# Storing the modulated input of the second block, and splitting projection inputs in the tile they are loaded into

## The chip, the cores and the metric

The kernel runs on one core of a Trainium2 chip. The metric is the time of one execution on the device in microseconds, as the median of several runs. The engines of a core run side by side, each through its own row of instructions in a fixed order: TensorE (PE, matmuls), VectorE (DVE), ScalarE (ACT), GpSimd (POOL) and SyncE (SP). In this kernel SP and POOL do hardly anything but issue transfers between the chip's memory and the core's tiles, and 16 DMA engines carry them out.

## The reference

One decoder layer for a sequence of 2048 tokens of width 1024, in float32. A conditioning vector gives a shift, a scale and a gate per channel for each of two sub-layers.

```python
def reference(x, c, w_ada, b_ada, w_in, conv_w, w_pool, pool_scale, w_out, ...):
    ...
        sh1, sc1, g1, sh2, sc2, g2 = jnp.split(mod, N_MOD, axis=-1)   # mod = silu(c) @ w_ada + b_ada
        h = x * (1.0 + sc1) + sh1            # the modulated input of this case
        z = h @ w_in[l]                      # 1024 -> 2048: the input projection
        ...                                  # gated short convolution and causal pooling of z
        mix = jnp.concatenate([y_conv, y_pool], axis=-1) @ w_out[l]
        x = _layer_norm(DEEPNORM_ALPHA * x + (1.0 + g1) * mix, ln1_g[l], ln1_b[l])
        h = x * (1.0 + sc2) + sh2
        f = jnp.square(jax.nn.relu(h @ w_mlp_in[l])) @ w_mlp_out[l]   # 1024 -> 4096 -> 1024
        x = _layer_norm(DEEPNORM_ALPHA * x + (1.0 + g2) * f, ln2_g[l], ln2_b[l])
```

The change touches how `h` of the first sub-layer gets into the product with `w_in`, for the second half of the tokens.

## The kernel before

**Blocks.** The 2048 tokens are worked on in two blocks of 1024 (`T`, `NB` = 2), one after the other: input projection with convolution and pooling, output projection and norm, MLP up, MLP down and norm. `xT` holds the input transposed, 8 tiles (`KD`) of 128 channels by 1024 tokens.

**Digits.** Every float32 operand is split into a high part, the value rounded to the format that PE takes (`F32R`), and a low part, what is left. A product is three matmuls in `mm3`: high by high (L153), high weight by low input (L154), low weight by high input (L155), each 128x128 by 128x512. `split` (and `parts`, for weights) makes the two: a cast on ACT (L146) and a subtraction on DVE (L147). So a weight tile costs a cast and a low part, and PE reads the low part from the third matmul on.

**Seven products.** The large matrix products are done in 2x2 blocks with seven block products in place of eight, as Strassen and Winograd do it. `seven` runs them in the order 0 to 6 in which they are called; one is 24 matmuls into two PSUM banks. The price is sums: of weight blocks, of input blocks and of results, made by DVE. In the MLP's first matrix (`up`) the hidden units come in 8 groups `g` (`NC` = 8). After each product `up` empties the banks with copies (`keep`, L1086), additions (`add`) or directly with an activation (`c21`, L1180, whose square is L1181); `join` is followed by the activation and the square, L1098 and L1099. The results' sums go to `usum` through POOL's queue.

**Tiles.** Tiles come from pools of fixed size, and one that asks for a slot waits until its last holder was read or stored: 10 for `o` (results and the side jobs), 6 for `w` (weight parts), 5 for `r` (what was loaded and is to be split), 28 for `h` (input parts).

**Side jobs.** The input projection of the second block also needs sums of its input blocks (`xsum`) and of its first weight (`winsum`). They are made while the first block's `up` runs. At the end of every product, `up` calls `beside`, which lets the side jobs advance by one beat: seven beats in a group. `first_side` starts four jobs `sum_x` at the beats 5, 11, 13 and 18 and two jobs `sum_first` at 20 and 26; `timed` starts a job's loads at its beat and runs the rest three beats later. `sum_x(k)` loads two tiles of `xT` into `o` tiles by POOL's queue, modulates them on ACT (L672), makes four differences of 128x512 on DVE in place and stores the two tiles to `xsum` by POOL's queue (L680).

**Preparing.** `prepare` is called through `turn` in the last group (`g` = 7), between its products 4 and 5. It loads and splits the first two weights and the first three inputs of the second block's projection; the further weights and inputs follow while the projection's first products run (`in_proj_1`). `inputs(X, key)` makes two tiles for each key; the keys with two digits are plain blocks (`xT`), those with one digit are sums (`xsum`). The load goes into an `r` tile by SP's queue (L705). A plain block is then modulated twice on ACT, once into the high part and once in place (four activations of 128x512, L712), and DVE subtracts; a sum goes through `split`. SP's queue also carries the weights' loads, L624 for this projection's.

The program that results has each engine's instructions in an order that a scheduler writes; the PE row near the last group's end holds some matmuls of the next projection's first product ahead of that group's product 6.

Of the kernel before, what the change touches and what calls it, by code (L numbers as in the profile page):

```python
# [8 lines left out]
F32 = mybir.dt.float32  # L9
F32R = mybir.dt.float32r  # L10
AF = mybir.ActivationFunctionType
ALU = mybir.AluOpType

P = 128
D = 1024
S = 2048
T = 1024
H = 512
NB = S // T
KD = D // P  # L20
# [80 lines left out]
SC1, SH1 = 0, 1  # L101
# [7 lines left out]
def tile_hybrid_layer(ctx: ExitStack, tc: tile.TileContext, opening, xT, x, wada, win,  # L109
                      wins, wpool, wout, wmix, w1, w2, rows, out):  # L110
    nc = tc.nc
# [11 lines left out]
    def mk(p, shape, dt, tag, bufs):  # L123
        names[0] += 1
        return p.tile(shape, dt, name=f"{tag}_{names[0]}", tag=tag, bufs=bufs)

    def t_h(dt=F32R):
        return mk(big, [P, T], dt, "h", 28)

    def t_o(w=T, dt=F32):  # L130
        return mk(big, [P, w], dt, "o", 10)
# [4 lines left out]
    def t_r():  # L136
        return mk(big, [P, T], F32, "r", 5)
# [7 lines left out]
    def split(src, hi, lo):  # L145
        high = nc.scalar.copy(hi, src)  # L146
        return high.ins, nc.vector.tensor_tensor(lo, src, hi.bitcast(F32), op=ALU.subtract).ins  # L147
# [15 lines left out]
    def tt(out_, a, b_, op):  # L163
        return nc.vector.tensor_tensor(out_, a, b_, op=op)  # L164
# [14 lines left out]
    halves = [slice(h * H, h * H + H) for h in range(2)]  # L179
# [24 lines left out]
    mod = cp.tile([P, 48], F32, name="mod")  # L204
# [46 lines left out]
    gout = tc.dram_tile([2, KD // 2, P, T], F32, name="gout")  # L251
    winsum = tc.dram_tile([4, P, T], F32, name="winsum")
    w1sum = tc.dram_tile([2, 4, P, T], F32, name="w1sum")
    xsum = tc.dram_tile([2, 4, P, T], F32, name="xsum")
    grow = tc.dram_tile([2, D], F32, name="grow")
    msum = tc.dram_tile([7, NG - 1, P, H], F32, name="msum")
# [409 lines left out]
    def sum_x(k):  # L666
        rs = [t_o() for _ in range(2)]
        for i, r in zip((k, k + 4), rs):
            nc.gpsimd.dma_start(r, xT[i])
        yield  # L670
        for i, r in zip((k, k + 4), rs):
            nc.scalar.activation(r, r, AF.Identity, bias=mod[:, 2 * i + SH1 : 2 * i + SH1 + 1],  # L672
                                 scale=mod[:, 2 * i + SC1 : 2 * i + SC1 + 1])
        (b11, b12), (b21, b22) = ((r[:, :H], r[:, H:]) for r in rs)
        tt(b12, b12, b11, ALU.subtract)
        tt(b22, b22, b12, ALU.subtract)
        tt(b11, b22, b11, ALU.subtract)
        tt(b21, b21, b22, ALU.subtract)
        for i, r in enumerate(rs):
            nc.gpsimd.dma_start(xsum[i, k], r)  # L680
# [13 lines left out]

    def inputs(X, key):
        for q in range(2):
            r = t_r()
            X[key, q] = hi, lo = t_h(), t_h()
            if len(key) == 1:
                src, hs = xsum[(int(key) + 1) % 2], halves[int(key) % 4 > 0 and int(key) < 3]  # L700
                k = 2 * q
            else:
                k, hs = 4 * int(key[0]) - 4 + 2 * q, halves[int(key[1]) - 1]
                src = xT
            nc.sync.dma_start(r.rearrange("p (a n) -> p a n", a=2),  # L705
                              src[k : k + 2, :, hs].rearrange("a p n -> p a n"))
            if len(key) == 1:
                split(r, hi, lo)
                continue
            for dst in (hi, r):  # L710
                for a, cs in enumerate(halves):
                    nc.scalar.activation(dst[:, cs], r[:, cs], AF.Identity,  # L712
                                         bias=mod[:, 2 * (k + a) + SH1 : 2 * (k + a) + SH1 + 1],
                                         scale=mod[:, 2 * (k + a) + SC1 : 2 * (k + a) + SC1 + 1])
            tt(lo, r, hi.bitcast(F32), ALU.subtract)

    def prepare():
        X = {}
        W = summed_weights(wins[0], winsum, (0, 1, 5, 4, 6, 7, 3))
        first_w = [parts(next(W), t_w)]  # L720
        for i in range(2):
            inputs(X, ORDER[i][1])
        first_w.append(parts(next(W), t_w))
        inputs(X, ORDER[2][1])
        return X, W, first_w

    def in_proj_1(X, W, first_w):
# [14 lines left out]
        def group(j):  # L742
# [11 lines left out]
            if j == 0:  # L754
                inputs(X, ORDER[3][1])
# [694 lines left out]
    def timed(jobs):  # L1450
        due = {}
        for beat in range(48):
            for _ in due.pop(beat, ()):
                pass
            if beat in jobs:
                next(jobs[beat])
                due[beat + 3] = jobs[beat]
            yield

    def first_side():  # L1460
        sums = [sum_x(n) for n in range(4)] + [sum_first(p) for p in halves]
        return timed(dict(zip((5, 11, 13, 18, 20, 26), sums)))

    def second_side():
        rows_ = [gate_dot(f) for f in range(G2, G2 + KD)] + [gate_row(), gate_back()]
        return timed(dict(zip((4, 6, 11, 13, 18, 20, 25, 27, 33, 37), rows_)))
# [93 lines left out]
```

## Time and profile before

| | |
|---|---|
| median of 3 runs | 1705.51 us (1705.37 to 1707.76) |
| profiled execution | 1707.25 us, of which the span is 1705.5 us |
| mean granted PE clock | 0.997 |
| moved by DMA | 469 MB, 275 GB/s on the mean |
| xsum stores | 8 of 512 KB, from 373.2 to 450.7 us |
| input loads for the second block (L705) | from 548.73 us on |

In the lines below, a row of the timeline has the start, the duration, the engine, the line and the operation with what is written and read; in brackets the idle time before it and what ended it. `x2` says that two such instructions follow each other. Instructions of one engine overlap a little, so the distance of two starts says more of the cost than the duration. A row of the waits has the total, the number and the longest. A row of DMA issues has the size and the median time from issue to landing. DVE is busy for 82% of the span and ACT for 49%, unevenly: the stages with sums fill DVE.

### The profile page before, as it was taken

What the parts mean: (1) busy time and instruction counts of PE and PEld (TensorE: products, weight loads), DVE (VectorE), ACT (ScalarE), POOL (GpSimd) and SP (SyncE); (2) the same over time, 40 slices, a digit from 0 to 9 for tenths busy, and PEclk for the clock granted to TensorE, in tenths of its full rate; (3) what the DMA queues carried; (4) which work ended last, traced back from release to release, by engine and by line L of the source; (5) the groups of instructions that cost most, each with busy time, mean ns of one, the idle gap of its engine ahead of it and who ended that gap; (6) DMA issues with size and microseconds to landing.
All of it is one profiled execution on the core that took longest, in us unless ns stands there. A gap on an engine that the chain in (4) does not pass through costs nothing.

```text
span 1705.5 us, 22025 instructions
## 1 busy us (share of the span) xinstructions
PE 1688.1 (99%) x7519; PEld 1396.8 (82%) x7519; DVE 1399.6 (82%) x2138; ACT 844.2 (49%) x1160; POOL 377.9 (22%) x687
## 2 busy tenths in 40 slices
PE   9999999999999899999999999999999999999998
PEld 7888888888888688888888888888888888888886
DVE  8898697888887586886888788766988887897898
ACT  6323358555554753345855454445543433334555
POOL 0222221445564122200145455430000000000000
PEclk9999999999999999999999999999999999999999
DMA  9998877668778778865889998899899999896782
GB/s 387 346 335 323 312 253 275 224 218 259 241 247 221 228 234 223 238 241 197 267 251 266 243 244 243 240 330 355 317 344 338 384 328 353 292 338 222 264 291 99
DMA packets 149217, 469.47 MB, mean 275 GB/s; under 512 B 20456, under 2 KB 20976, under 8 KB 149104
## 3 DMA queue, kind: packets, MB, share of 16 engines
q1 hardware_dynamic: 93184, 303.38, 50.5%
q0 software_dynamic: 55920, 164.67, 32.0%
q8 instruction: 59, 0.97, 0.3%
q14 instruction: 54, 0.44, 0.1%
HBM read 350.01 MB, written 159.91 MB: 299 GB/s over the span
## 4 chain that ended last, share of the span: by engine, by line
PE 90%; DVE 4%; DMA 3%; ACT 1%; issue 1%; POOL 0%; DVEq 0%; SPq 0%; ACTq 0%; POOLq 0%
PE ps L153 29%; PE ps L155 29%; PE ps L154 29%; PE ps L488 3%; DVE o L164 2%; DMA r<-in_xT 1%; PE ps L865 1%; DMA usum<-o 1%; DVE w L147 1%; DMA w<-in_w 1%; DVE r L164 0%; DMA wsum<-in_w 0%; DMA r<-in_w 0%; POOL usum L1111 0%; ACT w L146 0%
## 5 line engine op out<-in xcount | busy, mean ns | idle before, releaser
L153 PE MATMUL ps<-h,w 128*128 128x512 f32 x1312 | 511.9, 391 | 5.9 <-ACT w L146 4.2
L155 PE MATMUL ps<-h,w 128*128 128x512 f32 x1312 | 511.3, 390 | 0.5 <-DVE w L147 0.5
L154 PE MATMUL ps<-h,w 128*128 128x512 f32 x1312 | 511.7, 390 | 0.0
L153 PE MATMUL ps<-h,h 128*128 128x512 f32 (+1 forms) x1064 | 412.4, 388 | 0.9 <-DVE h L164 0.9
L154 PE MATMUL ps<-h,h 128*128 128x512 f32 (+1 forms) x1064 | 412.4, 388 | 0.9 <-DVE h L147 0.9
L155 PE MATMUL ps<-h,h 128*128 128x512 f32 (+1 forms) x1064 | 412.4, 388 | 0.0
L153 PEld LDWEIGHTS ps<-h,w 128*128 128x128 f32 x1312 | 246.9, 188 | 58.5 <-ACT w L146 4.7
L155 PEld LDWEIGHTS ps<-h,w 128*128 128x128 f32 x1312 | 246.7, 188 | 53.3 <-DVE w L147 1.7
L154 PEld LDWEIGHTS ps<-h,w 128*128 128x128 f32 x1312 | 247.1, 188 | 51.3
L1111 POOL DMA_DIRECT2D usum<-o x416 | 225.2, 550 | 254.2 <-DVE o L164 162.6
L146 ACT CAST w<-r 128x1024 fp32r<-128x1024 f32 x156 | 164.2, 1052 | 196.0 <-PE ps L154 190.4
L147 DVE TENSOR_TENSOR w<-r,w 128x1024 fp32r<-128x1024 f32 x156 | 190.6, 1223 | 59.9 <-ACT w L146 59.1
L146 ACT CAST h<-r 128x1024 fp32r<-128x1024 f32 (+1 forms) x136 | 136.5, 1009 | 198.6 <-PE ps L154 79.6
L154 PEld LDWEIGHTS ps<-h,h 128*128 128x128 f32 x1064 | 199.8, 188 | 42.1 <-DVE h L147 1.3
L153 PEld LDWEIGHTS ps<-h,h 128*128 128x128 f32 x1064 | 199.8, 188 | 42.0 <-DVE h L164 1.1
L155 PEld LDWEIGHTS ps<-h,h 128*128 128x128 f32 x1064 | 199.8, 188 | 40.9
L164 DVE TENSOR_TENSOR o<-o,o 128x256 f32<-128x256 f32 (+2 forms) x458 | 200.7, 491 | 2.7 <-ACT o L1099 1.1
L147 DVE TENSOR_TENSOR h<-r,h 128x1024 fp32r<-128x1024 f32 (+1 forms) x136 | 157.8, 1168 | 51.2 <-ACT h L146 51.0
L146 ACT CAST h<-w 128x1024 fp32r<-128x1024 f32 x104 | 109.1, 1049 | 104.9 <-DVE w L164 95.1
L147 DVE TENSOR_TENSOR h<-w,h 128x1024 fp32r<-128x1024 f32 x104 | 127.1, 1222 | 14.9 <-ACT h L146 14.7
L164 DVE TENSOR_TENSOR o<-o,ps 128x512 f32<-128x512 f32 x184 | 122.7, 684 | 19.2 <-PE ps L155 17.3
L164 DVE TENSOR_TENSOR o<-o 128x256 f32<-128x256 f32 (+1 forms) x176 | 82.6, 472 | 25.3 <-ACT o L1099 14.9
(166 smaller groups left out, 1424.7 us busy)
## 6 DMA issues: line engine op xcount, KB each, us to landing
usum<-o POOLq DMA_DIRECT2D x416, 128.0 KB, 5.2
r<-usum SPq DMA_DIRECT2D x104, 512.0 KB, 5.5
w<-wsum SPq DMA_DIRECT2D x76, 512.0 KB, 7.3
w<-in_w SPq DMA_DIRECT2D x72, 512.0 KB, 7.1
r<-in_w SPq DMA_DIRECT2D x68, 512.0 KB, 7.0
wsum<-in_w POOLq DMA_DIRECT2D x56, 512.0 KB, 7.6
wsum<-wsum POOLq DMA_DIRECT2D x24, 512.0 KB, 5.5
msum<-o POOLq DMA_DIRECT2D x18, 512.0 KB, 6.5
```

What stands on the lines that cost most here:

```text
L146: high = nc.scalar.copy(hi, src)
L147: return high.ins, nc.vector.tensor_tensor(lo, src, hi.bitcast(F32), op=ALU.subtract).ins
L153: nc.tensor.matmul(ps, whi, xhi, start=first, stop=False, skip_group_check=goes_on)
L154: nc.tensor.matmul(ps, whi, xlo, start=False, stop=False, skip_group_check=goes_on)
L155: done = nc.tensor.matmul(ps, wlo, xhi, start=False, stop=last, skip_group_check=goes_on)
L164: return nc.vector.tensor_tensor(out_, a, b_, op=op)
L488: nc.tensor.matmul(ps[m, h], wt[:, w : w + P], A[k][p // 2][:, hs], start=k == 0 and p == 0, stop=k == KD - 1 and p == 2)
L865: nc.tensor.transpose(ps[:, t * P : t * P + P], R[4 * h + t][:, k * P : k * P + P], ident)
L1111: nc.gpsimd.dma_start(usum[slot, g // 2, :, b, g % 2, :], z)
```

## The change

`sum_x` stores each tile to a new array `xmod` right after its modulation, by POOL's queue. It then yields once more, and `timed` gives such a job two further beats before it runs on: the four differences are made, in place as before, and the sums stored, two beats later than before. The jobs `sum_first` have no second yield and stay where they were. Since the differences overwrite the tiles, they wait until the stores to `xmod` have landed.

`inputs` no longer takes an `r` tile and no longer modulates. It loads `xmod` or `xsum` into the tile that will be the low part (`lo`, seen as float32) and calls `split` on it: one cast to the high part, and a subtraction that overwrites the tile with its low part.

```diff
--- before.py
+++ after.py
@@ -251,6 +251,7 @@
     gout = tc.dram_tile([2, KD // 2, P, T], F32, name="gout")
     winsum = tc.dram_tile([4, P, T], F32, name="winsum")
     w1sum = tc.dram_tile([2, 4, P, T], F32, name="w1sum")
+    xmod = tc.dram_tile([KD, P, T], F32, name="xmod")
     xsum = tc.dram_tile([2, 4, P, T], F32, name="xsum")
     grow = tc.dram_tile([2, D], F32, name="grow")
     msum = tc.dram_tile([7, NG - 1, P, H], F32, name="msum")
@@ -671,6 +672,8 @@
         for i, r in zip((k, k + 4), rs):
             nc.scalar.activation(r, r, AF.Identity, bias=mod[:, 2 * i + SH1 : 2 * i + SH1 + 1],
                                  scale=mod[:, 2 * i + SC1 : 2 * i + SC1 + 1])
+            nc.gpsimd.dma_start(xmod[i], r)
+        yield
         (b11, b12), (b21, b22) = ((r[:, :H], r[:, H:]) for r in rs)
         tt(b12, b12, b11, ALU.subtract)
         tt(b22, b22, b12, ALU.subtract)
@@ -694,25 +697,17 @@
 
     def inputs(X, key):
         for q in range(2):
-            r = t_r()
             X[key, q] = hi, lo = t_h(), t_h()
             if len(key) == 1:
                 src, hs = xsum[(int(key) + 1) % 2], halves[int(key) % 4 > 0 and int(key) < 3]
                 k = 2 * q
             else:
                 k, hs = 4 * int(key[0]) - 4 + 2 * q, halves[int(key[1]) - 1]
-                src = xT
+                src = xmod
+            r = lo.bitcast(F32)
             nc.sync.dma_start(r.rearrange("p (a n) -> p a n", a=2),
                               src[k : k + 2, :, hs].rearrange("a p n -> p a n"))
-            if len(key) == 1:
-                split(r, hi, lo)
-                continue
-            for dst in (hi, r):
-                for a, cs in enumerate(halves):
-                    nc.scalar.activation(dst[:, cs], r[:, cs], AF.Identity,
-                                         bias=mod[:, 2 * (k + a) + SH1 : 2 * (k + a) + SH1 + 1],
-                                         scale=mod[:, 2 * (k + a) + SC1 : 2 * (k + a) + SC1 + 1])
-            tt(lo, r, hi.bitcast(F32), ALU.subtract)
+            split(r, hi, lo)
 
     def prepare():
         X = {}
@@ -1450,11 +1445,13 @@
     def timed(jobs):
         due = {}
         for beat in range(48):
-            for _ in due.pop(beat, ()):
-                pass
+            for job in due.pop(beat, ()):
+                for _ in job:
+                    due.setdefault(beat + 2, []).append(job)
+                    break
             if beat in jobs:
                 next(jobs[beat])
-                due[beat + 3] = jobs[beat]
+                due.setdefault(beat + 3, []).append(jobs[beat])
             yield
 
     def first_side():
```

Five lines fewer stand above `up`, so L1086, L1098 and L1180 of before are L1081, L1093 and L1175 after; L680 becomes L683, L705 L708 and L624 L625.

ACT's row at the end of the last group's product 3 and in its product 4, before. `o_4882` takes product 4's banks (the copies L1086), `w_4911` is the cast of product 4's weight, `h_4971` and `r_4970` belong to the first input of the next projection.

```order
L146 CAST w_4911<-r_4763 128x1024
L712 ACTIVATE h_4971<-r_4970,mod 128x512
L1098 ACTIVATE o_4804<-o_4804 128x1024
L712 ACTIVATE h_4971<-r_4970,mod 128x512
L1099 ACTIVATE o_4804<-o_4804 128x1024
L712 ACTIVATE r_4970<-r_4970,mod 128x512
L1086 COPY o_4882<-ps_4773 128x512
```

The same place after; the copy of product 4's first bank is `o_4891`, product 4's weight is `w_4920`, and `h_4979`, `h_4984` and `h_4989` are the first three inputs' high parts.

```order
L146 CAST h_4979<-h_4980 128x1024
L146 CAST h_4984<-h_4985 128x1024
L146 CAST w_4920<-r_4772 128x1024
L1093 ACTIVATE o_4813<-o_4813 128x1024
L1094 ACTIVATE o_4813<-o_4813 128x1024
L146 CAST h_4989<-h_4990 128x1024
L1081 COPY o_4891<-ps_4782 128x512
```

Three casts of inputs, two of them ahead of the weight of product 4, stand where three half-tile modulations stood behind it.

ACT's row ahead of product 6's weight, before. That weight is `w_5048`; `w_5008` is a weight of the next projection and `r_4997` the fourth input.

```order
L712 ACTIVATE h_4998<-r_4997,mod 128x512 x2
L712 ACTIVATE r_4997<-r_4997,mod 128x512
L1098 ACTIVATE o_4915<-o_4915 128x1024
L712 ACTIVATE r_4997<-r_4997,mod 128x512
L1099 ACTIVATE o_4915<-o_4915 128x1024
L146 CAST w_5008<-r_5006 128x1024
L146 CAST h_5013<-r_5012 128x1024
L146 CAST w_5048<-r_4764 128x1024
```

And after, where product 6's weight is `w_5039`; `h_5005` and `h_5010` are high parts of inputs loaded from `xsum`, and `h_5135` that of the first input of the next key, loaded from `xsum` too.

```order
L1081 COPY o_4924<-ps_4907 128x512
L146 CAST h_5005<-h_5006 128x1024
L146 CAST h_5010<-h_5011 128x1024
L146 CAST w_5001<-r_4999 128x1024
L1093 ACTIVATE o_4924<-o_4924 128x1024
L1094 ACTIVATE o_4924<-o_4924 128x1024
L146 CAST h_5135<-h_5136 128x1024
L146 CAST w_5039<-r_4773 128x1024
```

The weight's cast stood behind modulations and one input loaded from the sums; it now stands behind three such inputs.

SP's queue in the last group, before, from the next projection's first weight on:

```order
L624 DMA r_4964<-in_wins 128x1024
L705 DMA r_4970<-in_xT 128x2x512
L705 DMA r_4979<-in_xT 128x2x512
L705 DMA r_4988<-in_xT 128x2x512
L705 DMA r_4997<-in_xT 128x2x512
L624 DMA r_5006<-in_wins 128x1024
L705 DMA r_5012<-xsum 128x2x512
L705 DMA r_5018<-xsum 128x2x512
L624 DMA r_5112<-winsum 128x1024
L705 DMA r_5144<-xsum 128x2x512
```

And after, where the load of `h_5136`, which ACT's cast `h_5135` above reads, is the last row:

```order
L708 DMA h_4980<-xmod 128x2x512
L625 DMA r_4973<-in_wins 128x1024
L708 DMA h_4985<-xmod 128x2x512
L625 DMA r_4999<-in_wins 128x1024
L708 DMA h_4990<-xmod 128x2x512
L625 DMA r_5103<-winsum 128x1024
L708 DMA h_4995<-xmod 128x2x512
L625 DMA r_5171<-winsum 128x1024
L708 DMA h_5006<-xsum 128x2x512
L708 DMA h_5011<-xsum 128x2x512
L625 DMA r_5232<-winsum 128x1024
L708 DMA h_5136<-xsum 128x2x512
```

Inputs go into `h` tiles and alternate with weights, which still go into `r` tiles; three weights of sums (`winsum`) stand between the fourth plain input and that load. On PE the matmuls of the next projection that stand ahead of the last group's product 6 are five where they were nine.

ACT's row where the side job that was begun at beat 13 ends, before. `o_3793` is `c21` of that group; it takes the slot of one of the job's two tiles, the first copy `o_3856` that of the other. `w_3896` is the weight of the next group's third product.

```order
L1098 ACTIVATE o_3620<-o_3620 128x1024
L1099 ACTIVATE o_3620<-o_3620 128x1024
L1180 ACTIVATE o_3793<-ps_3500 128x512
L1180 ACTIVATE o_3793<-ps_3513 128x512
L146 CAST w_3896<-r_3814 128x1024
L1181 ACTIVATE o_3793<-o_3793 128x1024
L1086 COPY o_3856<-ps_3826 128x512
L1086 COPY o_3856<-ps_3839 128x512
L146 CAST w_3944<-r_3891 128x1024
```

And after, with `o_3800`, `o_3863` and `w_3903` in these parts:

```order
L1093 ACTIVATE o_3619<-o_3619 128x1024
L1094 ACTIVATE o_3619<-o_3619 128x1024
L1175 ACTIVATE o_3800<-ps_3503 128x512
L1175 ACTIVATE o_3800<-ps_3516 128x512
L1176 ACTIVATE o_3800<-o_3800 128x1024
L1081 COPY o_3863<-ps_3833 128x512
L1081 COPY o_3863<-ps_3846 128x512
L146 CAST w_3903<-r_3821 128x1024
L146 CAST w_3947<-r_3898 128x1024
```

The weight's cast went from the place ahead of the square to the place behind the two copies. In POOL's queue the job's stores to `xmod` stand just ahead of the stores to `xsum` of the job before it, and its own stores to `xsum` stand behind the loads of the job after it; on DVE its differences come behind the sums out of the banks of that group's product 5. `c21` asks for the same slot as before.

## The prediction

> **What bounds the kernel now.** I read first the page's head and its share of busy time, then the list of TensorE's waits.
>
> ```profile
> span 1705.5 us, 22025 instructions
> PE 1688.1 (99%) x7519; PEld 1396.8 (82%) x7519; DVE 1399.6 (82%) x2138; ACT 844.2 (49%) x1160; POOL 377.9 (22%) x687
> PE ps L153 <- ACT w L146: 4.2, 1, 4.2
> PE ps L153 <- ACT o L1086: 1.7, 1, 1.7
> ```
>
> TensorE (PE) is busy for 99% of the span. A saving elsewhere is worth only what it takes out of a PE wait, and any new wait of PE is paid in full. The two waits shown are the largest, one occurrence each. The timeline of PE puts them into the last group of the MLP, where the next block's projection is prepared.
>
> ```profile
> 562.32 0.39 PE L155 MATMUL ps<-h,w 128*128 128x512 f32 x1
> 564.36 0.50 PE L153 MATMUL ps<-h,w 128*128 128x512 f32 x1 [1.65 <-ACT o L1086]
> ...
> 577.00 0.39 PE L154 MATMUL ps<-h,w 128*128 128x512 f32 x1
> 577.23 0.39 PE L155 MATMUL ps<-h,w 128*128 128x512 f32 x1
> 581.84 0.80 PE L153 MATMUL ps<-h,w 128*128 128x512 f32 x1 [4.23 <-ACT w L146]
> 582.43 0.63 PE L154 MATMUL ps<-h,w 128*128 128x512 f32 x1
> ...
> 587.55 0.47 PE L153 MATMUL ps<-h,w 128*128 128x512 f32 x1
> 588.32 0.39 PE L153 MATMUL ps<-h,w 128*128 128x512 f32 x1
> 582.00:590.00 8.00, 8.00 (x24) 6.39 (x25) 5.44 (x8) 2.50 (x3) 1.10 (x3) 0.64 0.96 302
> ```
>
> A matmul follows the last by 0.23 us before each wait (577.00 to 577.23). After the wait of 4.23 us PE goes on slowly until about 587.55; the last row, a window, shows a granted clock of 0.64. The 12 steps from 582.43 to 587.55 are 0.427 us each, so 12 x 0.20 = 2.4 us are lost. The place costs 1.65 + 4.23 + 2.4 = 8.3 us. ScalarE (ACT) is what both waits name:
>
> ```profile
> 559.72 0.82 ACT L712 ACTIVATE h<-r,mod 128x512 fp32r<-128x512 f32 x1 [7.02 <-DMA r<-in_xT]
> 563.74 0.56 ACT L1086 COPY o<-ps 128x512 f32<-128x512 f32 x1
> 574.15 1.51 ACT L712 ACTIVATE h<-r,mod 128x512 fp32r<-128x512 f32 x2
> 575.56 0.80 ACT L712 ACTIVATE r<-r,mod 128x512 f32<-128x512 f32 x1
> 579.80 1.04 ACT L146 CAST h<-r 128x1024 fp32r<-128x1024 f32 x1
> 580.75 1.04 ACT L146 CAST w<-r 128x1024 fp32r<-128x1024 f32 x1
> ```
>
> The modulation (L712) begins when its input lands, and the copy that empties a bank and the cast of product 6's weight (580.75) stand behind it in ACT's row.
>
> **The preparing stage.** Six input tiles lose four half-tile activations each and gain one cast. Two activations take 574.15 to 575.56, so 0.705 us each; a cast takes 0.95 (579.80 to 580.75). ACT is spared 6 x (4 x 0.705 - 0.95) = 11.2 us. VectorE's work is unchanged in count. The bytes loaded are the same; what changes is when a load may start, since its tile is no longer one of the five `r` but a low part that PE has finished reading.
>
> ```profile
> 548.73 19.38 SPq L705 DMA_DIRECT2D r<-in_xT  x4
> r<-in_xT SPq DMA_DIRECT2D x1, 512.0 KB, 11.0
> r<-in_xT SPq DMA_DIRECT2D x2, 512.0 KB, 4.8
> r<-xsum SPq DMA_DIRECT2D x5, 512.0 KB, 6.1
> ```
>
> Before, SP needs 19.4 us to issue four input loads because each waits for an `r`. The load issued at 548.73 takes 11.0 us, the two issued from 566.5 on take 4.8, and five loads of sums issued between 572 and 587 take 6.1. Product 4 was due right after 562.32, at 562.55; a product is 24 matmuls, 5.44 us, so the last group began four products earlier, at 540.8. After, the first two input loads wait only for PE's reads in that first product (its 17th and 23rd matmul), and can be issued near 545 and 546, 4 and 8 us sooner. The copy of 563.74 then stands behind three casts and no long modulation; even a landing after 11.0, at 556, leaves 6 us for them. I take **-1.65** for the first wait (0 to -1.65).
>
> Product 6's weight is another matter. Its cast now stands on ACT behind the cast of an input loaded from the stored sums. That load stands on SP's queue behind three weight loads, each of which still needs an `r`: one that product 4's low part frees, one that product 5's frees, one that the low part of the next projection's first weight frees. On ACT those stand behind the input casts. So three landings lie one behind another: 545 + 11.0 for the first input, then its cast, three low parts or sums on DVE and the next low part (1.0 + 1.2 + 0.6 + 1.2 + 1.2, by the rows of 579.80 and, further down, of 434.97 and 425.27), the fourth input's load (4.8), its cast, a copy, the weight's cast and low part (1.0 + 0.5 + 1.0 + 1.2), the sum's load (6.1), its cast and product 6's (2.0): 545 + 35.5 = 580.5, some of it side by side, say 579. PE wants it sooner than before: without the first wait, and with five matmuls of the next projection standing ahead of product 6 where nine stood, at 577.46 - 1.65 - 4 x 0.227 = 574.9. The wait stays about 4 and the slow stretch with it: **-0.2**. With quick landings (the first in 6.1, and 1 us off each of the others) it goes to nothing, the slow stretch included: -6.6. With landings 1 us longer it grows by 2.
>
> Of the clock the rows say that 1.65 us of waiting left it whole and 4.23 us did not. The Trainium skill, "TensorE: Matmul & The Clock Gate", Part 1, gives an idle window of about 3.4 us as what halves the rate; the two waits lie on its two sides. By that a wait of 4 keeps the slow stretch, and a wait of 3.3 would give the 2.4 us back, where the rows alone leave it open between 1.65 and 4.23.
>
> **The side jobs.** Each of four jobs now stores two modulated tiles, and only two beats later subtracts in place and stores the sums. Two more 512 KB stores per job, 4.2 MB in all, enter POOL's queue. Issuing the eight costs POOL 8 x 0.53 (the row of 421.30 below), and it has 2.5 us or more of each 10 free. Nothing of the jobs was in the way of PE before, as the full PE column shows.
>
> ```profile
> 420.00:430.00 10.00, 10.00 (x46) 8.27 (x45) 9.96 (x19) 7.04 (x9) 5.69 (x11) 1.00 0.69 204
> 430.00:440.00 10.00, 10.00 (x46) 8.29 (x45) 10.00 (x25) 4.08 (x6) 7.53 (x15) 1.00 0.94 277
> 440.00:450.00 10.00, 10.00 (x46) 8.28 (x45) 6.70 (x11) 8.30 (x10) 4.98 (x10) 1.00 1.05 318
> 460.00:470.00 10.00, 10.00 (x46) 8.29 (x45) 9.96 (x19) 6.64 (x8) 4.06 (x9) 1.00 0.29 107
> 421.30 1.07 POOL L680 DMA_DIRECT2D xsum<-o x2 [3.73 <-DVE o L164]
> xsum<-o POOLq DMA_DIRECT2D x2, 512.0 KB, 3.4
> xsum<-o POOLq DMA_DIRECT2D x2, 512.0 KB, 6.2
> xsum<-o POOLq DMA_DIRECT2D x2, 512.0 KB, 6.5
> ```
>
> The columns after the sum are PE, weight load, VectorE (DVE), ACT, POOL, granted clock, DMA share and GB/s. DVE is full in three of the four windows, and the DMA engines in two. The last rows are the stores of 421.30, 410.10 and 450.01. The job that stored at 421.30 is the one to look at: its tile is the slot that the group's last result takes next (`c21`, the pair of activations at 428.05 below), before as after. Before, the store landed 3.4 us after 421.3, well ahead of 428.05.
>
> ```profile
> 425.27 0.69 DVE L164 TENSOR_TENSOR o<-o,ps 128x512 f32<-128x512 f32 x1
> 426.54 1.23 DVE L147 TENSOR_TENSOR w<-r,w 128x1024 fp32r<-128x1024 f32 x1
> 428.05 1.06 ACT L1180 ACTIVATE o<-ps 128x512 f32<-128x512 f32 x2
> 429.00 1.05 ACT L146 CAST w<-r 128x1024 fp32r<-128x1024 f32 x1
> 430.90 0.59 ACT L1086 COPY o<-ps 128x512 f32<-128x512 f32 x1
> 434.97 1.22 DVE L147 TENSOR_TENSOR w<-r,w 128x1024 fp32r<-128x1024 f32 x1
> 437.92 0.39 PE L153 MATMUL ps<-h,w 128*128 128x512 f32 x1
> 438.37 0.39 PE L155 MATMUL ps<-h,w 128*128 128x512 f32 x1
> ```
>
> After, the subtractions follow the sum of 425.27. Three of them, a low part and a small sum, at some 0.6, 1.1 and 0.35 us, put the first store at 426 + 3.3 = 429.3 or a little later, say 429.6. It lands at 433.0 (3.4) to 436.1 (6.5). Behind it ACT has the pair (0.95), its square (0.95), two copies (0.5 each) and the cast that stood at 429.00 (1.05), which before stood ahead of square and copies and is for the next group's third product: 3.9 us; DVE's low part (the 434.97 row) adds 1.2. PE reads the cast at 437.92 and the low part at 438.37, so the wait is the landing + 5.1 - 438.4: from nothing to 2.8. The 430 to 440 window carries 0.94 of the DMA engines already, so I take 6.2: **+2.5**.
>
> *Contention.* At 318 GB/s, the rate of the fullest window, a 512 KB store is 1.65 us of all DMA engines, a pair 3.3. The pair now in 430 to 440, and the stores of the next job in 440 to 450, find no room. Two places x 3.3 is the upper bound; the lower is nothing, and no gain, since no byte is saved there. Half is **+3.3**. Should a wait reach 4.2 us there, 2.4 for the slow stretch come on top.
>
> *DVE.* The fourth job's four subtractions (2.4 us) must wait for its modulated store, which stands where the sums stood, near 450, and so lands near 456.5, and they hold up DVE's sums out of banks behind them. They also come into 460 to 470, which is full. Nothing to 2.4, I take **+1.2**; PE's next banks are due near 459.7 (437.92 + 4 products of 24 x 0.227), so their wait costs nothing to 2, I take **+0.5**.
>
> Here a rule speaks for the change. The Trainium skill, "DMA: Bandwidth & Descriptors", Anatomy of one DMA, gives 2.0 us + bytes/436e3, an estimated 3.2 for 512 KB; the row 3.4 agrees and the rows 6.2 and 6.5 do not: other transfers run beside those. By it the store lands at 432.8 and the +2.5 is zero.
>
> **The sum.** -1.65 - 0.2 + 2.5 + 3.3 + 1.2 + 0.5 = +5.65 us. The profiled run took 1707.25 us (span and 1.75 around it), 1.74 above the median of the three runs, 1705.51; the one gives 1712.9, the other **1711.2**, which I forecast, as a median will be measured. What a measurement can tell from no change is 0.2%, 3.4 us: below 1702.1 is faster, above 1708.9 slower.
>
> **Rivals.**
> *The stores are absorbed.* They land as the pair of 421.30 did (3.4) and the queues drain beside the work. The side terms vanish and -1.85 stays: 1703.7. For it: a DMA share of 0.69 and 0.29 in two of the four windows. Against: the other pairs took 6.2 and 6.5 without the added stores. 0.20.
> *The preparing stage comes free* (the other side). The first input lands in 6.1 and not 11.0, the chain to product 6's weight ends before 575, and 8.3 go. Without side waits 1697.2; with side waits of 7.5, 1704.7. It decides at the first input load: under about 7 us. For it: 11.2 us less ACT work and an earlier start; against: the three `r` loads in front of the sum's load, and a DMA share of 0.96 in the window at 582. 0.12 and 0.08.
> *Contention is heavy.* All 6.6 of it, and the slow stretch at one of the waits: 5.65 + 3.3 + 2.4, with the weight's wait 1 us longer and DVE's two terms at their ends (2.7 more): about +15, 1720.5. For it the shares 0.94 and 1.05; against, the free stretches on both sides of them, 0.69 and 0.29. 0.13.
>
> **How the numbers follow.** The forecast has 0.47; its own range, from its terms half taken to the bound of contention, is 1706 to 1716. The range 1697 to 1722 takes in the free stage without side waits (edge) and the heavy case with some more. Slower: 0.13 + 0.44 of the forecast = 0.57. Same: 0.16 of the absorbed, 0.08 of the free stage with side waits, 0.03 of the forecast = 0.27. Faster: 0.12 + 0.04 = 0.16.
>
> **What would show it.** In the changed profile's waits of PE: the copy's 1.7 gone, the weight cast's 4.2 near 4 and still followed by 0.43 us steps, and new ones between 430 and 485 on a weight's cast or low part of 1 to 4 us. In the DMA issues: xmod stores at 5 to 8 us and the sums' stores no quicker than now. I am wrong if PE is full from 360 to 540, if the weight's wait is under 1.6, or if a wait near 438 exceeds 5 us.

## The result, and the profile after

The changed kernel takes 1717.32 us (median of 4 runs, 1715.32 to 1721.98), the kernel before 1705.96 (4 runs): a ratio of 1.0069 with a 95% interval of 1.0046 to 1.0091, so 11.4 us slower. The forecast had been 1711.2 in a range of 1697 to 1722.

The spans of the two profiled executions differ by 9.2 us (1714.7 and 1705.5). The head of the page, TensorE's waits in PE's timeline, and one window of ten microseconds (the last three columns are granted clock, DMA share and GB/s), in the changed kernel:

```profile
span 1714.7 us, 22017 instructions
421.67 0.50 PE L153 MATMUL ps<-h,w 128*128 128x512 f32 x1 [0.99 <-DVE o L164]
444.08 0.79 PE L153 MATMUL ps<-h,w 128*128 128x512 f32 x1 [5.78 <-ACT w L146]
...
448.49 0.48 PE L153 MATMUL ps<-h,w 128*128 128x512 f32 x1
485.25 0.50 PE L153 MATMUL ps<-h,w 128*128 128x512 f32 x1 [0.44 <-ACT o L1081]
487.63 0.50 PE L155 MATMUL ps<-h,w 128*128 128x512 f32 x1 [1.65 <-DVE w L147]
575.34 0.50 PE L153 MATMUL ps<-h,w 128*128 128x512 f32 x1 [0.81 <-ACT o L1081]
591.76 0.58 PE L153 MATMUL ps<-h,w 128*128 128x512 f32 x1 [4.11 <-ACT w L146]
592.14 0.63 PE L154 MATMUL ps<-h,w 128*128 128x512 f32 x1
...
594.70 1.10 PE L155 MATMUL ps<-h,w 128*128 128x512 f32 x2
595.64 0.40 PE L153 MATMUL ps<-h,w 128*128 128x512 f32 x1
440.00:450.00 10.00, 5.88 (x16) 4.23 (x17) 7.71 (x15) 7.70 (x10) 7.50 (x14) 0.66 0.78 225
```

This accounts for the difference. From 444.08 to 448.49 PE takes nine steps in 4.41 us where 2.04 are normal, 2.4 lost; from 592.14 to 595.64 it takes eight steps in 3.5 us where 1.8 are normal, about 1.7 lost. The side jobs' stretch costs 0.99 + 5.78 + 2.4 + 0.44 + 1.65 = 11.3 us that was full before. The preparing stage costs 0.81 + 4.11 + 1.7 = 6.6, where it cost 8.3. Together +9.6, against 9.2 between the spans; the sum is good to a few tenths.

**The side jobs' place.** The rows of ScalarE, VectorE and POOL ahead of the wait of 5.78 us:

```profile
439.95 1.08 ACT L1175 ACTIVATE o<-ps 128x512 f32<-128x512 f32 x2 [8.49 <-DMA xsum<-o]
441.06 1.06 ACT L1176 ACTIVATE o<-o 128x1024 f32<-128x1024 f32 x1
442.03 1.05 ACT L1081 COPY o<-ps 128x512 f32<-128x512 f32 x2
442.97 2.95 ACT L146 CAST w<-r 128x1024 fp32r<-128x1024 f32 x3
```

```profile
415.94 0.69 DVE L164 TENSOR_TENSOR o<-o 128x512 f32<-128x512 f32 x1 [3.18 <-DMA xmod<-o]
420.32 0.69 DVE L164 TENSOR_TENSOR o<-o,o 128x512 f32<-128x512 f32 x1 [1.55 <-DMA xmod<-o]
428.59 0.68 DVE L164 TENSOR_TENSOR o<-o,ps 128x512 f32<-128x512 f32 x1
430.93 1.62 DVE L164 TENSOR_TENSOR o<-o,o 128x512 f32<-128x512 f32 x3
```

```profile
433.27 0.55 POOL L683 DMA_DIRECT2D xsum<-o  x1 [1.09 <-DVE o L164]
xsum<-o POOLq DMA_DIRECT2D x2, 512.0 KB, 6.5
```

ScalarE stands still for 8.49 us until the third job's first tile has been stored: `c21` wants its slot. The weight that PE needs for the next group's third product is the first of the three casts at 442.97, behind the pair, the square and two copies. PE has nothing to do from 438.3 to 444.08. The store was issued at 433.27, because VectorE had lost 3.18 and 1.55 us before, waiting for the second job's stores to `xmod` to land, and because the third job's differences come behind both sums out of the banks (the second is the row of 428.59).

**The preparing stage.** SP's first load, the landing times of the second and the third (the DMA issues between 558.5 and 560, and between 561 and 565 us), and ScalarE's casts that wait for the three and, last, that of product 6's weight:

```profile
556.65 0.38 SPq L708 DMA_DIRECT2D h<-xmod  x1
h<-xmod SPq DMA_DIRECT2D x1, 512.0 KB, 8.8
h<-xmod SPq DMA_DIRECT2D x1, 512.0 KB, 11.6
561.14 1.05 ACT L146 CAST h<-h 128x1024 fp32r<-128x1024 f32 x1 [1.58 <-DMA h<-xmod]
567.77 1.05 ACT L146 CAST h<-h 128x1024 fp32r<-128x1024 f32 x1 [5.58 <-DMA h<-xmod]
573.76 1.05 ACT L146 CAST h<-h 128x1024 fp32r<-128x1024 f32 x1 [1.92 <-DMA h<-xmod]
590.67 1.04 ACT L146 CAST w<-r 128x1024 fp32r<-128x1024 f32 x1
```

The first input is there 4.5 us after its issue (556.65 to 561.14), but the second takes 8.8 and the third 11.6. ScalarE's row has their casts ahead of product 4's weight and of product 2's copies (they empty the two banks that product 4 fills next), and so it idles for 5.58 us in the middle of the stage. Product 6's weight is cast at 590.67.

### The profile page after: what moved, and what is told of

The parts are those of the page before. It is cut to its first block, busy times and chain, and to the rows that moved or that the text cites. A ratio compares the mean times of both kernels' runs of the same rounds, so it can differ in the third digit from the quotient of the medians.

```text
span 1714.7 us, 22017 instructions
## 1 busy us (share of the span) xinstructions
PE 1690.6 (99%) x7519; PEld 1397.2 (81%) x7519; DVE 1400.2 (82%) x2138; ACT 834.5 (49%) x1142; POOL 382.4 (22%) x695
## 5 line engine op out<-in xcount | busy, mean ns | idle before, releaser
L146 ACT CAST h<-r 128x1024 fp32r<-128x1024 f32 (+1 forms) x128 | 128.1, 1006 | 194.5 <-PE ps L154 76.1
L147 DVE TENSOR_TENSOR h<-r,h 128x1024 fp32r<-128x1024 f32 (+1 forms) x128 | 147.9, 1162 | 48.7 <-ACT h L146 48.4
```

## The experiments

Each was timed in rounds beside the kernel before; the ratio is to that, with its 95% interval.

| run | what it is | us | ratio |
|---|---|---|---|
| e1 | side jobs' part alone | 1717.34 | 1.0067 (1.0055 to 1.0079) |
| e2 | delay alone | 1713.55 | 1.0046 (1.0034 to 1.0058) |
| e9 | delay of jobs 1 and 4 alone | 1706.24 | 1.0007 (0.9998 to 1.0016) |
| e12 | delay of job 3 alone | 1705.98 | 1.0009 (1.0000 to 1.0018) |
| e5 | delay alone, job 2 a beat earlier | 1710.62 | 1.0024 (1.0015 to 1.0033) |
| e6 | change, job 2 a beat earlier | 1716.01 | 1.0054 (1.0041 to 1.0067) |
| e3 | before, plain inputs into a third tile | 1708.37 | 1.0015 (1.0006 to 1.0023) |
| e4 | e3, prepared one product later | 1708.72 | 1.0017 (1.0008 to 1.0026) |
| e7 | before, with an order on ScalarE | 1699.11 | 0.9958 (0.9944 to 0.9971) |
| e10 | e7, prepared one product later | 1697.85 | 0.9963 (0.9951 to 0.9976) |
| e11 | change, with that order | 1711.09 | 1.0040 (1.0028 to 1.0053) |
| e8 | change, with that order, jobs 2 and 4 a beat earlier | 1704.45 | 0.9993 (0.9984 to 1.0001) |

The kernel before had medians of 1705.56 beside e1 to e4, 1705.34 beside e5 to e8 and 1704.54 beside the rest.

### Which part of the change costs

e1 keeps the changed `sum_x` and `timed` and takes `inputs` of the kernel before.

> Only the side jobs' part of the change: xmod is stored and the differences come two beats later, but the inputs of the projection are loaded and modulated as before, so xmod is read by nobody. Theory A (the loss is made by the side jobs alone, through landings that DVE and then the slot of c21 wait for): the waits near 422, 444 and 485 us come back, about 10.9 us with the slow stretch, and the preparing stage has its 8.3 us as before: 1716 to 1720. Rival (the loads of xmod share in the loss): 1706 to 1712.

The time and the side jobs' waits came out as theory A said: 1717.34 us, with waits of 1.51 us near 423, 5.86 near 445 and 1.64 near 488. So the loss is the side jobs'. It also means that splitting in place brought the whole kernel nothing that these runs can tell: 1717.3 with it and without it. One part of the expectation failed. The preparing stage did not keep its 8.3 us:

```profile
576.38 0.50 PE L153 MATMUL ps<-h,w 128*128 128x512 f32 x1 [0.83 <-ACT o L1089]
593.63 0.73 PE L153 MATMUL ps<-h,w 128*128 128x512 f32 x1 [4.04 <-ACT w L146]
```

With the inputs loaded and modulated as before, the stage has waits of 0.83 and 4.04 us, as in the whole change (0.81 and 4.11). The 1.7 us that the stage gained there can't be put down to the new way of making the inputs.

e2 takes the stores out as well.

```diff
-            nc.gpsimd.dma_start(xmod[i], r)
         yield
```

> As the run with the side jobs' part alone, without the stores to xmod: the differences and the stores to xsum come two beats later, and nothing waits for a landing of xmod. Theory A: DVE keeps its time, the store that c21 waits for is issued near 429.6 and not 433.3, lands at 433 to 436, and PE waits 0 to 2.8 us: 1706 to 1709. Rival (the two beats by themselves make the wait, the tile being held too long): 1713 to 1717.

Here theory A failed, and the rival's range held. 1713.55 us: without a byte more than before, the two beats of delay cost 8 us, and about 3.8 us (1717.34 - 1713.55) are the stores'. Rows of PE, VectorE, POOL and ScalarE in e2:

```profile
442.02 0.80 PE L153 MATMUL ps<-h,w 128*128 128x512 f32 x1 [4.91 <-ACT w L146]
417.43 1.23 DVE L164 TENSOR_TENSOR r<-r,r 128x1024 f32<-128x1024 f32 x1 [3.79 <-DMA r<-in_w]
431.51 1.06 POOL L682 DMA_DIRECT2D xsum<-o  x2
437.89 1.09 ACT L1182 ACTIVATE o<-ps 128x512 f32<-128x512 f32 x2 [8.19 <-DVE r L164]
```

There is no store to `xmod` to wait for, yet the store of the sums goes out at 431.51 and not at 429.6, and `c21` starts at 437.89, 6.4 us later. (The row names VectorE, which had long been done; by the time between them it is the store's landing that the activation waits for.) The differences of the second job now fall into the stretch of VectorE where the third's were, and the third's come behind it. VectorE also resumes later in it: at 417.43, after 3.79 us for the landing of a weight's load, where the kernel before resumed at 414.85 after 2.52:

```profile
414.85 1.23 DVE L164 TENSOR_TENSOR r<-r,r 128x1024 f32<-128x1024 f32 x1 [2.52 <-DMA r<-in_w]
```

### What in the delay costs

e9 and e12 let the extra `yield` only some jobs have, with nothing stored: the first and fourth (`k in (0, 3)`), or the third (`k == 2`).

> The delay alone (no stores to xmod, inputs as before), for the first and the fourth side job only; the second and the third finish as before. If the delay costs only where a held tile is asked for by PE's own chain, c21 and the copy behind it find their slots free and PE has no wait between 430 and 480: 1704 to 1707. Rival (four differences moved by two beats cost in DVE's full stretches wherever they are): 1708 to 1711.

> The complement: the delay alone, for the third side job only, the one whose two slots c21 and the first copy of the next group ask for. In the order that results the cast of the next group's third weight is ahead of c21's activation, so what is left is the copy's wait for the second slot: a wait of PE for that copy near 438 of 1 to 3 us, no slow stretch, 1706 to 1710. Rival (the wait of 4.9 us needs the other jobs' delays, and this one is hidden): 1704 to 1706 with PE full there.

e9: 1706.24 us, PE full from 420 to 470, a wait of 0.92 near 477: a delay where nobody asks for the tile costs little. e12: 1705.98, just under what was expected, and a wait for the copy of 0.52 where 1 to 3 had been. The rival, that the delay of this one job is hidden, is nearer. Rows of e12:

```profile
428.30 1.06 POOL L683 DMA_DIRECT2D xsum<-o  x2
434.75 1.09 ACT L1183 ACTIVATE o<-ps 128x512 f32<-128x512 f32 x2 [7.37 <-DMA xsum<-o]
437.71 0.50 PE L153 MATMUL ps<-h,w 128*128 128x512 f32 x1 [0.52 <-ACT o L1089]
```

The slot is waited for here too, 7.37 us of ScalarE's time. But the store leaves 3.2 us sooner than in e2 (428.30), and the scheduler left the cast ahead of the activation that waits. Of the 3.2 us, 2.7 are there when VectorE resumes after the weight's load (414.76, in e2 417.43); the second job's differences, which are not in this stretch, are the smaller part. PE loses 0.52 us for the copy, and 1.25 near 478. So neither the slot nor a single job's delay makes 8 us. Two things differ from e2, the late store and the weight's cast standing behind it; these two runs don't separate them.

e5 and e6 change one number, the second job's beat from 11 to 10, in e2 and in the whole change.

```diff
-        return timed(dict(zip((5, 11, 13, 18, 20, 26), sums)))
+        return timed(dict(zip((5, 10, 13, 18, 20, 26), sums)))
```

> The delay alone (no stores to xmod, inputs as before), with the second side job begun at beat 10 in place of 11. c21 asks for the same slot of the third job and waits for the same late store, but the order that results has the cast of the next group's third weight ahead of that activation on ACT and not behind it and two copies. If PE's wait of 4.9 us near 442 is the weight's cast standing behind the activation that waits: it goes with its slow stretch, 1704 to 1708. Rival (the late store or the delay as such costs the time): 1711 to 1715.

> The whole change with that one number changed, the second job at beat 10 in place of 11. The weight's cast is again ahead of the activation. Same theory: the wait of 5.8 us and its slow stretch go, the waits near 485 and the 4.1 us before product 6 stay, and the wait for the fourth job's store near 460 may grow to 2: 1707 to 1712. Rival (traffic of the stores decides): 1715 to 1719.

With the cast ahead, the weight's wait is gone in both. e5 missed its figure (1710.62, between the two ranges) and e6 did too (1716.01, in its rival's range). By the rows the next thing in ScalarE's row took the weight's place: the copy that empties the bank, behind the activation that waits. PE's rows near 440 of e5 and of e6:

```profile
438.62 0.50 PE L153 MATMUL ps<-h,w 128*128 128x512 f32 x1 [2.03 <-ACT o L1088]
```

```profile
441.01 0.79 PE L153 MATMUL ps<-h,w 128*128 128x512 f32 x1 [2.87 <-ACT o L1081]
```

By the ratios e5 is 0.22% below e2. But in e5 the third job's store also leaves 2.3 us sooner (429.24, in e2 431.51), so the cast's place is not the only thing that changed. In e6 the store leaves 0.55 sooner than in the change (432.72) and `c21` starts 1.6 sooner (438.31); PE's wait goes from 5.78 to 2.87, so about 1.3 us of it speak for the cast's place. e6's time, 0.15% below the change, cannot be told from it, as their intervals overlap; it kept the waits near 485, with a slow stretch behind them, and its wait before product 6 was 4.5.

### What the preparing stage's 8.3 us are

e3 tests whether the five `r` tiles are to blame. One line of `inputs` of the kernel before is changed:

```diff
-            r = t_r()
+            r = t_r() if len(key) == 1 else t_h(F32)
```

> The kernel before, its side jobs untouched and its four activations for each plain input kept; only the tile is another: a plain input is loaded into a third tile of the pool of input parts (read by no matmul) and not into one of the five r. Theory A for the preparing stage (the 8.3 us are made by loads that wait for r tiles, so that modulations start late and bunch up): the loads start near 545 us and the waits of 1.65 and 4.23 us with the slow stretch shrink to under 2 us: 1697 to 1701. Rival (the 11 us of ACT's work that the change spares are what PE waits for): 1704 to 1707.

Neither: 1708.37 us. Rows of e3, the first two of SP's issues, the third of the DMA issues between 546 and 553 us, the rest of ScalarE and PE:

```profile
545.02 0.38 SPq L705 DMA_DIRECT2D h<-in_xT  x1
549.30 0.84 SPq L705 DMA_DIRECT2D h<-in_xT  x1
h<-in_xT SPq DMA_DIRECT2D x1, 512.0 KB, 14.4
563.76 0.81 ACT L712 ACTIVATE h<-h,mod 128x512 fp32r<-128x512 f32 x1 [5.18 <-DMA h<-in_xT]
565.10 0.50 PE L153 MATMUL ps<-h,w 128*128 128x512 f32 x1 [2.20 <-ACT o L1086]
```

The loads do start near 545 and 549, and the second then takes 14.4 us to land, at 563.7. In the kernel before it was issued 4.7 us later (553.98) and had landed at 561.5, 7.5 us on. ScalarE waits for it with a modulation that stands ahead of product 2's copy, and PE waits 2.20 for that copy. The wait before product 6 did shrink, from 4.23 to 1.92. Two further waits of 1.16 and 1.49 came in near 615 us, in the second block's projection.

> The same as the run with a third tile, and the preparation is begun one product later, after product 5 of the last group. If product 6's weight waits behind what preparing puts in front of it on ACT, nothing is left of the waits: 1696 to 1699. Rival: the projection of the second block then starts on inputs that are not ready, and waits some 2 to 6 us there: 1700 to 1704.

e4, with `turn` one product later, made 1708.72: the wait before product 6 is gone, the copy's 1.92 is still there, and 1.44 and 2.42 us come in the projection. The mechanism of that expectation's rival is there; the time lies above its range too.

e7 leaves loads, tiles and activations of the kernel before as they are, and adds an order on ScalarE alone: what `prepare` puts there comes behind `kept`, the last copy of product 2's banks in that group.

```diff
+            kept = mark[0]
             beside(mark[0])
             product(3, Z, True)
...
-                ready.append(prepare())
+                with ordered(ins):
+                    ready.append(prepare())
```

> The kernel before with one thing added: what prepare puts on ACT may not stand ahead of the copies that empty product 2's banks in the last group. The loads, the r tiles and the activations are the same. If the preparing stage's 8.3 us come from the place that the modulations have in ACT's row, ahead of copies and casts that PE needs: both waits shrink to under 1.5 together, 1697 to 1701. Rival (the landing of the inputs or ACT's work decides): 1704 to 1707.

1699.11 us, 6.2 below the kernel before beside it. ScalarE's and PE's rows of e7:

```profile
558.05 0.58 ACT L1096 COPY o<-ps 128x512 f32<-128x512 f32 x1
559.21 1.52 ACT L722 ACTIVATE h<-r,mod 128x512 fp32r<-128x512 f32 x2 [0.58 <-DMA r<-in_xT]
578.63 0.50 PE L153 MATMUL ps<-h,w 128*128 128x512 f32 x1 [0.50 <-ACT w L146]
603.22 0.50 PE L155 MATMUL ps<-h,w 128*128 128x512 f32 x1 [1.05 <-DVE w L147]
```

The second copy of product 2's banks runs at 558.05, and the modulations fill ScalarE behind the copies. In the kernel before it stood at 565.15:

```profile
565.15 0.58 ACT L1086 COPY o<-ps 128x512 f32<-128x512 f32 x1
```

The same 24 modulations and the same five `r` tiles leave PE waits of 0.50 and 1.05 in place of 8.3. So the stage's loss in the kernel before was the place of the modulations in ScalarE's row, not their work.

> The kernel before with the order on ACT as in the run with order alone, and the preparation begun one product later. If the 0.5 us before product 6 is still the preparation's work on ACT, it goes and nothing comes in its place: 1697 to 1699. Rival (the second block's projection waits for its inputs): 1700 to 1703.

e10 came out as expected: 1697.85 us, with no wait of PE in its timeline between 362 and 1131. It is the fastest of these kernels, and has nothing of the change in it. Its interval overlaps that of e7.

### The change with both places mended

> The whole change, with prepare's casts not ahead of product 2's copies on ACT, and the side jobs as the change has them. If the preparing stage and the side jobs cost independently, the 0.8 and 4.1 us and the slow stretch behind product 5 go and the waits near 422, 444 and 485 stay: 1708 to 1712. Rival (the later side waits shift the stage so that other waits come in): 1713 to 1717.

e11, 1711.09 us, is 0.29% below the change by the ratios, some 5 us, and e7 is 0.42% below the kernel before. Its waits of 1.15, 5.74 and 1.35 us in the side jobs' stretch stayed; in the preparing stage the copy's wait is gone and 1.46 is left before product 6. By the rows the two places cost independently, near enough.

> The whole change with both: second and fourth job begun a beat earlier (10 and 17), and the input casts of prepare not ahead of product 2's copies on ACT. If the two places are all that the change costs, PE keeps at most a wait of some 2 us near 480: 1697 to 1703, faster than before. Rival (the 4.2 MB of stores cost by themselves): 1708 to 1713.

e8, 1704.45 us, is the change with the order of e7 and two jobs a beat earlier. It is level with the kernel before (0.9993), above the 1697 to 1703 that had been expected and below the rival's range, and 5.3 us above e7, which does without `xmod`. PE's rows in e8:

```profile
439.07 0.50 PE L153 MATMUL ps<-h,w 128*128 128x512 f32 x1 [1.85 <-ACT o L1091]
439.97 0.63 PE L153 MATMUL ps<-h,w 128*128 128x512 f32 x1
...
442.96 0.48 PE L154 MATMUL ps<-h,w 128*128 128x512 f32 x1
```

The copy's wait for the third job's second tile is left, with a slow stretch of 3 us behind it. No wait of PE over 1 us is left near 420 or 485. So most of what the change lost can be had back with the stores in place. Whether the stores themselves are then free is not shown, since no run holds the tiles in this order without them.

## Why the prediction was right, and where its sum was not

Direction and place held, and the time fell into the range: slower, through waits near 440 and 480, with the weight's wait before product 6 left at about 4. But one of the prediction's own signs of being wrong came true. It named a wait near 438 of more than 5 us, and PE stood still for 5.78 us from 438.3 on. So the mechanism of the largest wait was right and its size was not. The forecast's own range, 1706 to 1716, was missed as well; the range of 1697 to 1722 held because it took in the case of heavy contention, whose mechanism is not what came. That part is luck. Of a sum of +5.65 us the chip made +11.4, and the terms did not fail evenly.

- **The slot of `c21`, +2.5 (0 to 2.8): measured 5.78 and 2.4 of slow stretch.** The mechanism was the one forecast, down to the names. The step that failed is the time of the store, 429.6 forecast and 433.27 measured: VectorE was assumed to reach the sum ahead of the differences when it did before, at 425.27. The change moved rows ahead of it too. In e2, without any store to `xmod`, that sum comes at 426.83 and POOL has two loads in front of the store, 1.9 us in all. In the change the sum comes another 1.76 later (428.59), behind VectorE's waits for the stores to `xmod`. The landing itself was 6.2 forecast and 6.5 measured. The slow stretch was named as a price on top and should have been in the sum, since a wait of 4 us was only 1.5 away.
- **Contention, +3.3: the stores cost 3.8, but not in that way.** The median landing of the eight stores of sums is 6.0 before and 4.5 after, so they did not get slower. By the rows the 3.8 us came through VectorE, which the differences in place make wait for each `xmod` store: e1 has waits of 1.51 near 423 and 1.64 near 488 that e2 has not, and waits 0.95 longer for the weight (5.86 and 4.91). That the figure fits is luck. No run stores to `xmod` from tiles that are not overwritten, so contention is not ruled out as a part.
- **VectorE's lag, +1.2 and +0.5: measured 0.44 + 1.65 near 485 and nothing near 460.** The size was right, and half of the place. The 0.99 near 421, behind the landings of the second job's stores to `xmod`, has no term in the forecast.
- **The first wait, -1.65: measured 0.81 left.** One of the three casts ahead of the copy waited for the third input's landing of 11.6 us. What did go is not the new inputs' doing, as e1 has 0.83 there with the old ones.
- **Product 6's weight, -0.2: measured 4.11, with some 0.7 us less of slow stretch.** Right in size, for a reason that was half right. The chain of the prediction is added up wrongly: the terms it lists make 32.8 us and not 35.5, so it ends at 577.8, and the wait by it is under 3. And the first landing was quick, 4.5 us, and by the forecast's own condition (under about 7) the stage should then have come free. The second and third were slow, and their casts block ScalarE in the same way. That rival's deciding point was wrongly chosen; e7, and for the change e11, show the real one, the order on ScalarE.
- **Heavy contention, 1720.5.** The time came near it, by another mechanism.

What stays open: no run delays the second and third job alone, and none changes the cast's place with the store's time held, so how the 8 us of the delay divide between the late store and the cast is argued from rows; why the weight's load in e2 lands later was not followed; why the scheduler puts the cast ahead in e5, e6 and e12 and behind in the change was not tried by itself; and the 5.3 us between e8 and e7 are explained by rows only as far as the 1.85 us and the slow stretch go.

## What to carry to other kernels

When a job's tile is held longer, ask who takes its slot next and what stands behind that instruction on its engine: PE waited for a cast that had no part in the job at all. Beginning an input stage earlier on a full DMA queue need not land its inputs earlier (the second load of e3, issued 4.7 us sooner, landed 2.2 us later); put an order on the engine that shares them with PE's own chain first, which here brought 6 us without any change of work. And an update in place behind a store turns the store's landing into a wait of the engine that updates.

## What the runs showed of the hardware

The slow stretch does not go by the length of the wait alone. In e8 it follows a wait of 1.85 us, and begins 0.9 us after it (439.97); in e5 a wait of 2.03 us is followed by steps of 0.23 us, and in the kernel before one of 1.65 is too. The prediction left it open between 1.65 and 4.23, and these runs put cases of both kinds close to 2 us. What lies shortly before a wait may count too: in e6 waits of 0.81 and 1.65 us follow each other (482.28 and 484.66) and the clock falls, while in the change waits of 0.44 and 1.65 in the same place leave steps of 0.23 behind them. What decides is not shown. The Trainium skill, "TensorE: Matmul & The Clock Gate", Part 1, gives about 3.4 us of idling; the 1.85 us of e8 is well below that, and the measurement decides. Windows of e8, e6 and e5, with the granted clock third from the end:

```profile
440.00:442.00 2.00, 2.00 (x6) 1.61 (x5) 1.97 (x7) 2.00 (x3) 1.42 (x3) 0.50 1.09 301
```

```profile
484.00:488.00 4.00, 3.34 (x8) 2.67 (x9) 4.00 (x5) 2.72 (x3) 3.08 (x5) 0.60 0.74 265
```

```profile
438.00:444.00 6.00, 5.38 (x24) 4.45 (x25) 5.57 (x13) 2.95 (x4) 4.30 (x8) 1.00 1.02 257
```

A 512 KB load took from 4.5 us (after) to 14.4 us (e3) in the same stage. The share of the DMA engines does not tell the two apart: it was 1.01 while the first was on its way and 1.04 while the second was. What does was not measured. For transfers that GpSimd issues, the Trainium skill, "DMA: Bandwidth & Descriptors", Anatomy of one DMA, would make 512 KB an estimated 3.2; the stores of the third job, which GpSimd issued, took 6.5, and the measurement decides here too.
